# Seven block products for eight in four more places, and the last K tiles of a pair put last

## The chip, the cores and the metric

The kernel runs on one core of a Trainium2 chip. The metric is the device time of one execution in microseconds (us). The core has a matrix engine (TensorE, PE in the rows; its weight loads are PEld), a vector engine (VectorE, DVE), a scalar engine (ScalarE, ACT), a general engine (GpSimd, POOL) and a queue engine (SyncE, SP). Each works through its own queue in order; they wait for each other by semaphores. Weights and activations travel by DMA between device memory and the on-chip buffer, issued here from SP's and from POOL's queue.

## What is computed

Two blocks follow each other on x of 256 tokens x 2048 features, all in float32. The first block is two hybrid layers (banded attention, gated linear attention and attention to a memory). The change is in the second block, which in short is:

```python
h = rms_norm(x, norm_mix_pre)
proj = h @ w_in
a_q, a_f, a_i, a_g, b_q, b_k, b_v, b_f, g_a, g_b = jnp.split(proj, split_points, axis=-1)
y_a = hgrn2_mixer(a_q, a_f, a_i, a_g, lb, hgrn_norm_w) @ w_up_a
y_b = fox_mixer(b_q, b_k, b_v, b_f + b_fox_f) @ w_up_b
merged = sigmoid(g_a) * y_a + sigmoid(g_b) * y_b
x = x + rms_norm(merged @ w_o, norm_mix_post)
h = rms_norm(x, norm_ffn_pre)
gate, up = jnp.split(h @ w_ffn_in, 2, axis=-1)          # 2 x 5632 columns
x = x + rms_norm((silu(gate) * up) @ w_ffn_down, norm_ffn_post)
```

The HGRN2 mixer is a recurrence with a decay per feature, done in chunks of 64 tokens for 8 heads; the FoX mixer is a causal softmax attention with a forget gate, for 8 heads. g_a and g_b, the merge's gates, are 2048 columns each.

## The kernel before

**Products.** A float32 product is made of three matmuls on halves of less precision. Each operand x is split into a high part (a rounding copy) and a low part (x minus the high part), and `three` (L439) adds high·high, high·low and low·high into one accumulator (L441 to L443). For weights the high part is a cast on ACT (L356) and the low part a subtraction on DVE (L357); activations and other on-chip tiles are split the same way by `split_to` (L506, L507).

**Work units.** `Builder.run` (L249) goes through a list of jobs. A job is a group of up to 512 columns against all its K tiles of 128 rows, for the two token halves. It takes two K tiles at a time: one tile of weights (128 x 1024 floats, a "slot"), split into two slots, feeds 2 K tiles x 2 token halves x 3 = 12 matmuls of 128 x 512. Such a step is called a unit here. The accumulators of a job are a "main" tile of two banks, of which there are two; smaller products go to four single banks.

**Slots.** All tiles on chip of this size come from one pool of 41 slots. `ahead` (L370) loads raw weights on SP up to four ahead and splits up to six parts ahead of the unit that needs them, as long as enough slots are free. If they are not, `run` makes the split directly ahead of its unit, in the loop that begins with `while split <= i`. The order in which instructions are written down is the order of each engine's queue.

**Side work.** The heads of both mixers, the normalisations, the merging and the hidden activations are generators. `pump` (L229) advances up to two of them after each unit, by due times counted on a clock of matmul work. In the stretch of the merge's gates the HGRN heads (`hgrn_head`, L924) do, for each of two token halves of a head: the differences of the decays on POOL (`decay_levels`, L839: L846 to L856), two passes on ACT for the exponential (L857, L858), fourteen multiplications on POOL (L938, L939) and a reduction on DVE (L957), besides small products on PE. The FoX heads run in the same stretch, with their softmax on DVE and ACT (L786 to L791).

**Seven for eight.** `Shared` (L79) is a pair of two 512-column jobs a and b on the same activations. On one quad of K tiles (two K halves) the pair is a product of 2 x 2 blocks (token halves, K halves) with 2 x 2 blocks (K halves, the columns of a and of b): eight block products of 2 K tiles x 3 = 6 matmuls each. It is done with seven, by sums of blocks. The seven are called d, a, c, T1, T2, T4 and T3; the four T ones come after everything else of the pair. The sums of weight blocks are made by `sums` (L317) with four accumulating DMAs on POOL's queue (`add`, L303 and L304), each of which waits for the one before it: three (a += b, b += d, d += a) when a is split, and c += d when c is split. The raw tiles of the quad stay in their slots until the T products are split. The sums of activation blocks are made once per activation by `combos_of` (L616): four or five additions on POOL, one operation on DVE, and a split. The results leave the accumulators by copies on ACT (L462, L484, L491) and additions on DVE (L486 to L488, L493 to L497). Before, only the FFN's gate and up pairs do this, on K tiles 12 to 15.

**Order of the jobs.** gates gb0 to gb3 (each post, L1532, a tanh on ACT), the four jobs of w_up_b, gates ga0 to ga2, the last columns of w_in, ga3, w_up_a, then w_o (`residual_jobs`, L1614), then the FFN in three groups of 4, 4 and 3 pairs of 512 hidden columns, each followed by its part of w_ffn_down (four jobs; the last group's through `residual_jobs`).

Of the kernel before, what the change touches and what calls it, by code (L numbers as in the profile page):

```python
# [78 lines left out]
class Shared:  # L79
# [453 lines left out]
def network(ctx, tc, a):  # L533
# [82 lines left out]
    def combos_of(get2, quad):  # L616
# [13 lines left out]
        B.release([xi, ci])  # L630
        return ids

    def parted(ids):
# [893 lines left out]
    def post_gate(key, c):  # L1527
# [5 lines left out]
        return post  # L1533

    def post_upb(c):
        def post(ps):
# [29 lines left out]
    merging = {}  # L1566

    def merged(c):
# [4 lines left out]
        B.release([st[f"gb{c}"]])  # L1573

    def merged_get(kt):
# [7 lines left out]
    for g in range(2):  # L1583
# [29 lines left out]

    def residual_jobs(label, w_, post_row, resid, done, act_, order, k0=0, partial=None, pre1=None):  # L1614

# [31 lines left out]
        def finish(t):  # L1647
# [6 lines left out]
            done(q["r"], t)  # L1654

        n = len(order) // 2
        for c in range(4):
            jobs.append(Job("x", w_, 512 * c, 512, act_, post(c), order=order, k0=k0,
                            pre={0: begin, 1: pre1, 2: load_x}.get(c), apart=(label, n - 4 if c == 2 else 0, n) if c > 1 else None))

# [3 lines left out]
    def mix_done(ids, t):  # L1664
# [13 lines left out]
        else:  # L1678
            def done():
                B.release(ids + f["wi"])  # L1680
                f["make"] = make_fcombos()
                B.start(f["make"])
            start_late(fact, [f[0], f[1]], x1res, None, done, False)

    def pre_w2():
# [3 lines left out]
    residual_jobs("o", a["w_o_2"][0], a["norm_mix_post_2"][0], tokens(xres), mix_done, Act(merged_get), range(NKT),  # L1689
                  pre1=pre_w2)  # L1690

# [27 lines left out]

    QUADS = [(12, 13, 14, 15)]  # L1720

    def make_fcombos():
        for quad in QUADS:
            f.setdefault("combos", []).append(combos_of(lambda k: B.act[:, k:k + 2], quad))
            yield 3000

    def fcombos(q):
        if f["make"] in B.side:
            B.drain([f["make"]])
        return parted(f["combos"][q])  # L1730

    def post_both(c):

        def post(gi, ui):
# [3 lines left out]
            if f["units"] * 512 == D_FF:  # L1738
                B.release(sum(f["combos"], []))
        return post  # L1740

    def hidden(c, gi, ui=None):
# [15 lines left out]
        B.release([gi])  # L1758

    def hidden_get(kt):  # L1760
# [6 lines left out]

    def post_part(c, new):
        def post(ps):
            if c == 0 and new:  # L1770
                f["part"] = B.alloc(4)
            p = s(f["part"][c])
            if new:
                V.tensor_copy(p, flat(ps))
            else:
                V.tensor_tensor(p, p, flat(ps), ALU.add)
        return post

    def out_done(ids, t):
# [5 lines left out]
    for g, n in enumerate((4, 4, 3)):  # L1785
        for c in range(n):
            c0 = 512 * (at + c)
            head = (g, c) == (0, 0)
            if not head:
                std = range(16 - 4 * len(QUADS))  # L1790
                gate = Job("x", wf, c0, 512, fact, lambda ps: None, order=std, open=(1,))
                up = Job("x", wf, D_FF + c0, 512, fact, lambda ps: None, order=std)
                jobs.append(Shared(gate, up, QUADS, fact, fcombos, post_both(c)))
                continue
# [3 lines left out]
        if g < 2:  # L1798
            for c in range(4):
                jobs.append(Job("x", a["w_ffn_down_2"][0], 512 * c, 512, hact, post_part(c, g == 0), order=order, k0=k0))  # L1800
        else:
            residual_jobs("down", a["w_ffn_down_2"][0], a["norm_ffn_post_2"][0], tokens(x1res), out_done, hact, order, k0,
                          partial=lambda: f["part"])
        at += n
# [54 lines left out]
```

## Time and profile before

| | |
|---|---|
| median of 3 runs | 2400.83 us (2399.18 to 2401.85) |
| profiled execution | 2401.03 us |
| its span | 2399.3 us |
| PE busy | 2380.5 us, 99% of the span |
| DVE busy | 1566.2 us, 65% |
| ACT busy | 1160.0 us, 48% |
| POOL busy | 441.5 us, 18% |
| accumulating DMAs on POOL (L304) | 40, 512 KB each |

The span is the time from the first to the last record of the profile; the profiled execution's own time is 1.7 us longer. The busy time of PE counts matmuls whose ends are modelled and which overlap, so it is not a measure of how full the engine is; how far apart the starts of two matmuls are, tells more. The rows give start, duration, engine, line, operation, the tile written and the tiles read, and in square brackets the idle time of the engine ahead of the row and what ended it.

### The profile page before, as it was taken

To read this page: it belongs to the slowest core of one execution; us is meant where nothing else is said; L and a number is where in the kernel's file an instruction comes from. 1 tells how busy PE (TensorE), PEld (TensorE's weight loads), DVE (VectorE), ACT (ScalarE), POOL (GpSimd) and SP (SyncE) were. 2 spreads that over 40 slices of the span, in tenths; PEclk is the share of its full clock that TensorE was granted. 3 is DMA by queue.
4 is the path that set the end of the run, shared out by engine and by line. 5 is a ranking of instruction groups with operands and counts; after the bars stand their busy time and mean duration, and the time that the engine had idled before them with its cause. 6 is when DMAs were issued, how large, how long until landed. Compare 5 with 4: busy or idle time off the path is not lost. (4 is left out here: it accounts for less than half of the span.)

```text
span 2399.3 us, 31682 instructions
## 1 busy us (share of the span) xinstructions
PE 2380.5 (99%) x12045; PEld 2005.0 (84%) x12045; DVE 1566.2 (65%) x1783; ACT 1160.0 (48%) x1553; POOL 441.5 (18%) x646
## 2 busy tenths in 40 slices
PE   9999999999999999999999999999999999999998
PEld 7888888888888888888888888888888888888876
DVE  6587567566865667766775655657567557665675
ACT  5444455345454553655554434445555445544553
POOL 0330010004400110354754440001100000000000
PEclk9999999999999999999999999999999999999999
DMA  9545567674556574944654556675877578767773
GB/s 329 184 147 187 167 188 261 205 244 141 176 167 187 189 256 148 295 154 128 193 160 151 199 185 193 196 243 171 274 229 224 190 209 261 228 215 226 223 241 131
DMA packets 319672, 485.62 MB, mean 202 GB/s; under 512 B 22600, under 2 KB 162208, under 8 KB 319520
## 3 DMA queue, kind: packets, MB, share of 16 engines
q1 hardware_dynamic: 312528, 459.48, 58.8%
q0 software_dynamic: 6400, 23.07, 4.9%
q8 instruction: 94, 1.54, 0.3%
q10 hardware_dynamic: 592, 1.06, 0.1%
q14 instruction: 58, 0.48, 0.1%
HBM read 454.18 MB, written 8.40 MB: 193 GB/s over the span
## 5 line engine op out<-in xcount | busy, mean ns | idle before, releaser
L357 DVE TENSOR_TENSOR slot<-slot,slot 128x1024 fp32r<-128x1024 f32 x770 | 967.0, 1292 | 266.6 <-ACT slot L356 253.0
L356 ACT CAST slot<-slot 128x1024 fp32r<-128x1024 f32 x770 | 774.4, 1047 | 299.8 <-PE main L442 94.5
L428 PE MATMUL main<-act,slot 128*128 128x512 f32 x1824 | 651.2, 400 | 0.0
L441 PE MATMUL main<-slot,act 128*128 128x512 f32 x1488 | 589.5, 396 | 0.7 <-ACT slot L356 0.7
L442 PE MATMUL main<-slot,act 128*128 128x512 f32 x1488 | 580.0, 390 | 1.6 <-DVE slot L357 1.6
L443 PE MATMUL main<-slot,act 128*128 128x512 f32 x1488 | 580.3, 390 | 0.0
L429 PE MATMUL main<-act,slot 128*128 128x256 f32 x1824 | 510.0, 280 | 0.0
L428 PEld LDWEIGHTS main<-act,slot 128*128 128x128 f32 x1824 | 342.5, 188 | 80.3 <-issue 1.1
L429 PEld LDWEIGHTS main<-act,slot 128*128 128x128 f32 x1824 | 344.2, 189 | 0.8
L443 PEld LDWEIGHTS main<-slot,act 128*128 128x128 f32 x1488 | 279.3, 188 | 59.2
L442 PEld LDWEIGHTS main<-slot,act 128*128 128x128 f32 x1488 | 279.7, 188 | 58.3 <-DVE slot L357 2.8
L441 PEld LDWEIGHTS main<-slot,act 128*128 128x128 f32 x1488 | 279.6, 188 | 57.3 <-ACT slot L356 1.1
L441 PE MATMUL main<-slot,slot 128*128 128x512 f32 x620 | 244.2, 394 | 0.7 <-ACT slot L506 0.7
L443 PE MATMUL main<-slot,slot 128*128 128x512 f32 x620 | 242.6, 391 | 0.0
L442 PE MATMUL main<-slot,slot 128*128 128x512 f32 x620 | 242.1, 390 | 0.0
L304 POOL DMA_DIRECT2D slot<-slot x40 | 35.0, 874 | 563.4 <-DMA slot<-in_w_ffn_in_dram 196.8
L443 PEld LDWEIGHTS main<-slot,slot 128*128 128x128 f32 x620 | 116.8, 188 | 25.8 <-DVE slot L507 1.3
L441 PEld LDWEIGHTS main<-slot,slot 128*128 128x128 f32 x620 | 116.9, 188 | 25.3 <-ACT slot L506 1.4
L442 PEld LDWEIGHTS main<-slot,slot 128*128 128x128 f32 x620 | 116.8, 188 | 23.4
L507 DVE TENSOR_TENSOR slot<-slot,slot 128x1024 fp32r<-128x1024 f32 (+1 forms) x91 | 98.6, 1102 | 33.5 <-ACT slot L506 33.5
L846 POOL TENSOR_TENSOR slot<-slot 128x128 f32<-128x128 f32 x144 | 79.2, 581 | 192.3 <-PE main L428 93.2
L506 ACT CAST slot<-slot 128x1024 fp32r<-128x1024 f32 (+1 forms) x91 | 85.1, 956 | 47.0 <-DMA slot<-slot 16.5
(225 smaller groups left out, 1987.0 us busy)
## 6 DMA issues: line engine op xcount, KB each, us to landing
slot<-in_w_in_dram SPq DMA_DIRECT2D x384, 512.0 KB, 3.8
slot<-in_w_ffn_in_dram SPq DMA_DIRECT2D x176, 512.0 KB, 4.9
slot<-in_w_ffn_down_dram SPq DMA_DIRECT2D x88, 512.0 KB, 4.8
slot<-in_w_out_dram SPq DMA_DIRECT2D x64, 512.0 KB, 4.8
slot<-slot POOLq DMA_DIRECT2D x40, 512.0 KB, 7.2
slot<-in_w_o_dram SPq DMA_DIRECT2D x32, 512.0 KB, 4.7
slot<-in_w_mem_kv_dram SPq DMA_DIRECT2D x31, 512.0 KB, 6.4
slot<-in_w_up_b_dram SPq DMA_DIRECT2D x16, 512.0 KB, 4.6
```

The costliest lines, as they stand in the source:

```text
L304: nc.gpsimd.dma_start(self.s(out), self.s(x), accum_op=ALU.add)
L356: nc.scalar.copy(h, src)
L357: nc.vector.tensor_tensor(l, src, h.bitcast(F32), ALU.subtract)
L428: nc.tensor.matmul(job.ps[:, f, :], h[:, k, fs], xs, start=st, stop=False)
L429: nc.tensor.matmul(job.ps[:, f, :S], l[:, k, fs], xh, start=False, stop=en)
L441: nc.tensor.matmul(o, xh, h, start=start, stop=False)
L442: nc.tensor.matmul(o, xh, l, start=False, stop=False)
L443: nc.tensor.matmul(o, xl, h, start=False, stop=stop)
L506: nc.scalar.copy(h, src)
L507: nc.vector.tensor_tensor(l, src, h.bitcast(F32), ALU.subtract)
L846: G.tensor_tensor(view(E[:, l, :]), view(bt), ref, ALU.subtract)
```

## The change

- A pair's order (`Shared.sequence`): the last four K tiles of both jobs (two units each) are moved behind everything else but the T products. This holds for every pair, the FFN's too.
- `Combos` and `shared_pair` are new helpers: the sums of activation blocks as a generator, and a pair made of two jobs.
- Gates gb2 and gb3 become a pair, and ga0 and ga1, on K tiles 12 to 15, with sums of activation blocks that are made once when the second half of the FoX heads is started and kept until the second pair is done. Their tanh then works in place on the pair's results.
- w_o: columns 0 and 1 become a pair on K tiles 0 to 3.
- w_ffn_down: in the first and second group, columns 0 and 1 and columns 2 and 3 become pairs on the group's first four K tiles. In the third group columns 0 and 1 become a `Shared` without a quad: no product is left out, and only the order of the units differs.

```diff
@@ Shared.sequence
-        rest = slice(2, None)
-        seq = own(self.b, slice(0, 1)) + mine("d") + own(self.b, slice(1, 2)) + mine("a") + own(self.b, rest)
-        seq += own(self.a, slice(0, 1)) + mine("c") + own(self.a, slice(1, None))
+        seq = own(self.b, slice(0, 1)) + mine("d") + own(self.b, slice(1, 2)) + mine("a") + own(self.b, slice(2, -2))
+        seq += own(self.a, slice(0, 1)) + mine("c") + own(self.a, slice(1, -2))
+        seq += own(self.b, slice(-2, None)) + own(self.a, slice(-2, None))
...
+    def shared_pair(w_, cs, act_, order, combos, post, pres=(None, None), k0=0):
+
+        std = [k for k in order if k not in combos.quad]
+        ja, jb = (Job("x", w_, c, 512, act_, lambda ps: None, order=std, k0=k0, pre=pre, open=op)
+                  for c, pre, op in zip(cs, pres, ((1,), ())))
+        return Shared(ja, jb, [combos.quad], act_, combos, post)
...
     def start_f(g):
         B.drain([gens["bf"]])
+        if g == 1:
+            gcombos.start()
...
+    gcombos = Combos(lambda k: B.act[:, k:k + 2], (12, 13, 14, 15))
+
+    def post_gates(key, c, last):
+        def post(*ids):
+            for e, i in enumerate(ids):
+                st[f"{key}{c + e}"] = i
+                for t in range(2):
+                    A.activation(vt(i)[:, t, :], vt(i)[:, t, :], AF.Tanh, scale=rs2h[:, t:t + 1])
+            if last:
+                gcombos.release()
         return post
...
-    for c in range(4):
-        X(9224 + 512 * c, 512, act, post_gate("gb", c))
+    X(9224 + 512 * 0, 512, act, post_gate("gb", 0))
+    X(9224 + 512 * 1, 512, act, post_gate("gb", 1))
+    jobs.append(shared_pair(w, (9224 + 512 * 2, 9224 + 512 * 3), act, range(NKT), gcombos, post_gates("gb", 2, False)))
...
-    for c in range(3):
-        X(7176 + 512 * c, 512, act, post_gate("ga", c))
+    jobs.append(shared_pair(w, (7176 + 512 * 0, 7176 + 512 * 1), act, range(NKT), gcombos, post_gates("ga", 0, True)))
+    X(7176 + 512 * 2, 512, act, post_gate("ga", 2))
...
+        if combos:
+            jobs.append(shared_pair(w_, (0, 512), act_, order, combos, both, (pre1, begin), k0))
+        else:
+            one, two = (Job("x", w_, 512 * c, 512, act_, post(c), order=order, k0=k0, pre=pre)
+                        for c, pre in ((0, pre1), (1, begin)))
+            jobs.append(Shared(one, two, [], act_, None, None))
...
-            for c in range(4):
-                jobs.append(Job("x", a["w_ffn_down_2"][0], 512 * c, 512, hact, post_part(c, g == 0), order=order, k0=k0))
+            for c in (0, 2):
+                jobs.append(shared_pair(a["w_ffn_down_2"][0], (512 * c, 512 * c + 512), hact, order, Hidden(),
+                                        post_parts(c, g == 0), k0=k0))
```

The diff adds one line ahead of most of the code, so `decay_levels`' first line L846 is L875 after the change, L857 is L886, L304 is L305, and `three` is L442 to L444.

**The gates, POOL's queue.** slot_9910 holds a head's decays. Before, at the decay of a token half in gb2 (slot_11613), with the last multiplication of the half ahead of it:

```order
L944 TENSOR_TENSOR slot_11314<-slot_11314,slot_10191 128x128
L599 TENSOR_TENSOR rs_11608<-rs_11608,nhalf 128x1
L846 TENSOR_TENSOR slot_11613<-slot_9910 128x128 x6
L849 TENSOR_SCALAR slot_11613<-slot_9910 128x64
L850 COPY slot_11613<-slot_9910 128x64
L855 COPY slot_11613<-slot_9910 128x64
L856 TENSOR_SCALAR slot_11613<-slot_9910 128x64
L938 TENSOR_TENSOR slot_11613<-slot_11613,slot_9909 128x64
```

And now, where the same half is slot_11597, and slot_11403, 11379, 11330 and 11554 are the raw tiles a, b, d and c of the pair gb(2,3):

```order
L973 TENSOR_TENSOR slot_11311<-slot_11311,slot_10191 128x128
L305 DMA slot_11403<-slot_11379 128x1024
L305 DMA slot_11379<-slot_11330 128x1024
L305 DMA slot_11330<-slot_11403 128x1024
L875 TENSOR_TENSOR slot_11597<-slot_9910 128x128 x6
L878 TENSOR_SCALAR slot_11597<-slot_9910 128x64
L879 COPY slot_11597<-slot_9910 128x64
L884 COPY slot_11597<-slot_9910 128x64
L885 TENSOR_SCALAR slot_11597<-slot_9910 128x64
L600 TENSOR_TENSOR rs_11657<-rs_11657,nhalf 128x1
L305 DMA slot_11554<-slot_11330 128x1024
L967 TENSOR_TENSOR slot_11597<-slot_11597,slot_9909 128x64
```

Three accumulating DMAs now stand between the multiplications of one half and the decay of the next. In the second pair, ga(0,1), all four stand in a row ahead of the decay of slot_12429, and ACT's cast of slot_12442 (a unit of the pair's second accumulator, main_12510) behind that decay's exponentials.

**The gates, ACT's queue, at the same place.** Before (slot_11650 is a weight that PE uses four units later):

```order
L356 CAST slot_11586<-slot_11521 128x1024
L864 ACTIVATE sc_11511,ss_11607<-bank_11604 128x128
L857 ACTIVATE slot_11613<-slot_11613 128x1024
L858 ACTIVATE slot_11613<-slot_11613 128x1024
L796 COPY P_11402<-bank_11638 128x384
L356 CAST slot_11650<-slot_11527 128x1024
L356 CAST slot_11668<-slot_11546 128x1024
```

And now (slot_11610, 11662, 11681 and 11705 are weights of the pair's second accumulator, main_11635):

```order
L886 ACTIVATE slot_11597<-slot_11597 128x1024
L887 ACTIVATE slot_11597<-slot_11597 128x1024
L357 CAST slot_11610<-slot_11537 128x1024
L825 COPY P_11489<-bank_11648 128x384
L893 ACTIVATE sc_11545,ss_11656<-bank_11653 128x128
L507 CAST slot_11662<-slot_11554 128x1024
L507 CAST slot_11027<-bank_11675 128x256
L357 CAST slot_11681<-slot_11560 128x1024
L357 CAST slot_11705<-slot_11583 128x1024
```

PE's queue, now, at those weights; the units' other products are left out:

```order
L526 MATMUL bank_11629<-slot_11311 128x128 x4
L442 MATMUL main_11635<-slot_11610,act 128x512
...
L530 MATMUL bank_11648<-ident,P_11489 128x128 x3
L526 MATMUL bank_11653<-slot_8285,sc_11545 128x128
L526 MATMUL bank_11653<-slot_8285,cross_11547 128x128
L442 MATMUL main_11635<-slot_11662,act 128x512
...
L526 MATMUL bank_11675<-P_11428,slot_10537 128x128 x3
L442 MATMUL main_11635<-slot_11681,act 128x512
...
L526 MATMUL bank_11699<-slot_11311 128x128 x3
L526 MATMUL bank_11699<-slot_10191,slot_9909 128x128
L442 MATMUL main_11635<-slot_11705,act 128x512
```

Each of these weights is now cast after ACT or DVE has read a bank that PE fills directly ahead of the weight's unit. On DVE the subtractions of slot_11681 and slot_11705 stand behind such reads in the same way; that of slot_11786, five units on, stands behind a subtraction that reads a bank and behind the reduction of L986 (L957 before).

**The last group of down, PE's queue.** Before, column 0 is main_19495, and slot_19419 holds the last hidden columns, which are transposed here:

```order
L441 MATMUL main_19495<-slot_19453,slot_15408 128x512
...
L529 MATMUL bank_19576<-ident,slot_19419 128x128 x4
L529 MATMUL bank_19583<-ident,slot_19419 128x128 x4
L441 MATMUL main_19495<-slot_19467,slot_15752 128x512
```

And now, with column 0 in main_19821, column 1 in main_19748 and the last hidden columns in slot_19672:

```order
L442 MATMUL main_19748<-slot_19706,slot_15521 128x512
...
L442 MATMUL main_19821<-slot_19779,slot_15521 128x512
...
L530 MATMUL bank_19902<-ident,slot_19672 128x128 x4
L530 MATMUL bank_19909<-ident,slot_19672 128x128 x4
L442 MATMUL main_19748<-slot_19797,slot_15877 128x512
```

Four units of the second column now stand ahead of the transposes.

Counted over the whole program, PE has 42 matmuls fewer (11512 in place of 11554, as written down), DVE 81 more tensor-tensor operations, POOL 20 more, and POOL's queue 28 more DMAs.

## Rows read from the trace of the kernel before

**Rows 1.** The page: busy time and share of the span, for each engine

```profile
PE 2380.5 (99%) x12045; PEld 2005.0 (84%) x12045; DVE 1566.2 (65%) x1783; ACT 1160.0 (48%) x1553; POOL 441.5 (18%) x646
```

**Rows 2.** Waits of PE: what waited for what, total us, times, longest us

```profile
PE bank L529 <- DVE slot L1750: 2.5, 2, 1.4
PE bank L529 <- DVE sc L866: 1.7, 1, 1.7
```

**Rows 3.** PE's timeline in an FFN group's down, first and last of 46 products

```profile
1899.80 0.39 PE L441 MATMUL main<-slot,slot 128*128 128x512 f32 x1
...
1910.00 0.39 PE L441 MATMUL main<-slot,slot 128*128 128x512 f32 x1
```

**Rows 4.** PE's timeline in the last group, at the transposes

```profile
2329.04 0.39 PE L443 MATMUL main<-slot,slot 128*128 128x512 f32 x1
...
2332.27 0.99 PE L529 MATMUL bank<-ident,slot 128*128 128x128 f32 x7 [1.12 <-DVE slot L1750]
2333.49 0.50 PE L441 MATMUL main<-slot,slot 128*128 128x512 f32 x1 [0.24 <-ACT slot L506]
...
2337.35 0.40 PE L441 MATMUL main<-slot,slot 128*128 128x512 f32 x1
```

**Rows 5.** Stretches: length, busy PE, PEld, DVE, ACT, POOL, PEclk, DMA share, GB/s

```profile
2333.40:2337.40 4.00, 3.91 (x10) 2.82 (x11) 2.52 (x3) 1.47 (x3) 0.00 (x0) 0.57 0.54 203
...
1137.20:1141.00 3.80, 3.74 (x23) 3.23 (x23) 3.80 (x4) 2.85 (x4) 3.80 (x5) 1.00 0.86 259
```

**Rows 6.** The stretch of one FFN gate and up pair, columns as before

```profile
1796.70:1839.90 43.20, 43.20 (x196) 35.73 (x196) 31.32 (x34) 23.40 (x29) 3.52 (x4) 1.00 0.80 225
```

**Rows 7.** POOL's timeline over one FFN pair's accumulating DMAs

```profile
1972.93 0.87 POOL L304 DMA_DIRECT2D slot<-slot  x1 [32.15 <-DMA slot<-in_w_ffn_in_dram]
1978.75 0.87 POOL L304 DMA_DIRECT2D slot<-slot  x1 [4.95 <-PE main L442]
1988.57 0.87 POOL L304 DMA_DIRECT2D slot<-slot  x1 [8.96 <-DMA slot<-slot]
1996.98 0.87 POOL L304 DMA_DIRECT2D slot<-slot  x1 [7.54 <-issue]
```

**Rows 8.** POOL's timeline in gb2, at a decay

```profile
1304.59 0.55 POOL L599 TENSOR_TENSOR rs<-rs,nhalf 128x1 f32<-128x1 f32 x1 [9.82 <-DVE rs L598]
1305.10 2.21 POOL L846 TENSOR_TENSOR slot<-slot 128x128 f32<-128x128 f32 x6
```

**Rows 9.** ACT's timeline at the same place

```profile
1303.95 0.28 ACT L864 ACTIVATE sc<-bank 128x128 f32<-128x128 f32 x1 [3.61 <-PE bank L525]
...
1308.55 1.06 ACT L857 ACTIVATE slot<-slot 128x1024 f32<-128x1024 f32 x1 [4.23 <-POOL slot L856]
...
1310.97 1.05 ACT L356 CAST slot<-slot 128x1024 fp32r<-128x1024 f32 x1
```

**Rows 10.** DVE's timeline in gb2: a normalisation, a softmax's first row, the next

```profile
1287.95 0.29 DVE L866 TENSOR_TENSOR sc<-bank,rs 128x128 f32<-128x128 f32 x1 [0.69 <-POOL rs L599]
...
1289.88 0.29 DVE L786 CUSTOM_DVE_ANT_0 P<-bank,P 128x128 f32<-128x128 f32 x1
...
1292.65 1.23 DVE L357 TENSOR_TENSOR slot<-slot,slot 128x1024 fp32r<-128x1024 f32 x1
```

**Rows 11.** DMA issues: tiles, queue, count, KB each, median us to landing

```profile
slot<-in_w_in_dram SPq DMA_DIRECT2D x384, 512.0 KB, 3.8
...
slot<-slot POOLq DMA_DIRECT2D x40, 512.0 KB, 7.2
```

**Rows 12.** DVE by line, 1240 to 1470: count, busy us, mean ns, idle before

```profile
L357 DVE TENSOR_TENSOR slot<-slot,slot 128x1024 fp32r<-128x1024 f32 x76 | 93.4, 1251 | 31.6 <-ACT slot L356 31.2
L957 DVE TENSOR_REDUCE sc<-slot 128x128 f32<-128x1024 f32 x8 | 16.0, 2003 | 0.0
L954 DVE TENSOR_TENSOR slot<-bank,slot 128x512 f32<-128x512 f32 x16 | 11.0, 689 | 14.9 <-PE bank L525 14.9
```

**Rows 13.** ACT by line, the same stretch and columns

```profile
L506 ACT CAST slot<-bank 128x256 fp32r<-128x256 f32 x4 | 1.5, 371 | 7.0 <-PE bank L525 7.0
```

More of the change, by code (lines that the diff above doesn't have):

```diff
@@ L631, in combos_of, with __init__, start, gen @@
         return ids
+    class Combos:
+        def __init__(self, get2, quad):
+            self.get2, self.quad = get2, quad
+        def start(self):
+            def gen():
+                self.ids = combos_of(self.get2, self.quad)
+                yield
+            self.gen = gen()
+            B.start(self.gen)
+        def __call__(self, q):
+            if self.gen in B.side:
+                B.drain([self.gen])
+            return parted(self.ids)
+        def release(self):
+            B.release(self.ids)
+    def shared_pair(w_, cs, act_, order, combos, post, pres=(None, None), k0=0):
[3 more added lines that the diff above has]
+        return Shared(ja, jb, [combos.quad], act_, combos, post)
     def parted(ids):
@@ L1533, in post_gate @@
         return post
+    gcombos = Combos(lambda k: B.act[:, k:k + 2], (12, 13, 14, 15))
[7 more added lines that the diff above has]
+                gcombos.release()
+        return post
     def post_upb(c):
@@ L1566, in network @@
     merging = {}
+    FIRST = (0, 1, 2, 3)
+    ocombos = Combos(lambda k: B.act[:, k:k + 2], FIRST)
     def merged(c):
@@ L1573, in merged @@
         B.release([st[f"gb{c}"]])
+        if c == 1:
+            ocombos.start()
     def merged_get(kt):
@@ L1611, in network, with residual_jobs @@
                         pre=B.settle if c == 0 else None))
-    def residual_jobs(label, w_, post_row, resid, done, act_, order, k0=0, partial=None, pre1=None):
+    def residual_jobs(label, w_, post_row, resid, done, act_, order, combos, k0=0, partial=None, pre1=None):
         q = {}
@@ L1654, in finish, with both @@
             done(q["r"], t)
-        n = len(order) // 2
-        for c in range(4):
+        def both(i0, i1):
+            for c, i in enumerate((i0, i1)):
+                post(c)(vt(i))
+            B.release([i0, i1])
+            combos.release()
+        n = len(order) // 2
+        if combos:
[4 more added lines that the diff above has]
+            jobs.append(Shared(one, two, [], act_, None, None))
+        for c in (2, 3):
             jobs.append(Job("x", w_, 512 * c, 512, act_, post(c), order=order, k0=k0,
-                            pre={0: begin, 1: pre1, 2: load_x}.get(c), apart=(label, n - 4 if c == 2 else 0, n) if c > 1 else None))
+                            pre=load_x if c == 2 else None, apart=(label, n - 4 if c == 2 else 0, n)))
     fact = row_act(lambda: B.release(xsrc["ids"]))
@@ L1680, in done @@
                 B.release(ids + f["wi"])
-                f["make"] = make_fcombos()
-                B.start(f["make"])
+                fcombos.start()
             start_late(fact, [f[0], f[1]], x1res, None, done, False)
@@ L1689, in network @@
     residual_jobs("o", a["w_o_2"][0], a["norm_mix_post_2"][0], tokens(xres), mix_done, Act(merged_get), range(NKT),
-                  pre1=pre_w2)
+                  ocombos, pre1=pre_w2)
     wf = a["w_ffn_in_2"][0]
@@ L1718, in post_up2 @@
         return post
[L1720 to L1730, printed above, removed]
+    fcombos = Combos(lambda k: B.act[:, k:k + 2], (12, 13, 14, 15))
+    hcombos = []
     def post_both(c):
@@ L1738, in post @@
             if f["units"] * 512 == D_FF:
-                B.release(sum(f["combos"], []))
+                fcombos.release()
         return post
@@ L1758, in hidden @@
         B.release([gi])
+        if c == 1 and f.setdefault("groups", 0) < 2:
+            f["groups"] += 1
+            hcombos.append(Combos(lambda k: kx(f["h"][k // 2]), FIRST))
+            hcombos[-1].start()
     def hidden_get(kt):
@@ L1766, in network, with post_parts, post, __call__ @@
     hact = Act(hidden_get)
[L1768 to L1776, printed above, removed]
-        return post
+    def post_parts(c, new):
+        def post(*ids):
+            for e, i in enumerate(ids):
+                if new:
+                    f.setdefault("part", {})[c + e] = i
+                else:
+                    V.tensor_tensor(s(f["part"][c + e]), s(f["part"][c + e]), s(i), ALU.add)
+                    B.release([i])
+            if c == 2:
+                hcombos.pop().release()
+        return post
+    class Hidden:
+        quad = FIRST
+        def __call__(self, q):
+            return hcombos[-1](q)
     def out_done(ids, t):
@@ L1789, in network @@
             if not head:
[L1790 to L1793, printed above, removed]
+                jobs.append(shared_pair(wf, (c0, D_FF + c0), fact, range(NKT), fcombos, post_both(c)))
                 continue
@@ L1798, in network @@
         if g < 2:
-            for c in range(4):
-                jobs.append(Job("x", a["w_ffn_down_2"][0], 512 * c, 512, hact, post_part(c, g == 0), order=order, k0=k0))
-        else:
-            residual_jobs("down", a["w_ffn_down_2"][0], a["norm_ffn_post_2"][0], tokens(x1res), out_done, hact, order, k0,
-                          partial=lambda: f["part"])
+            for c in (0, 2):
+                jobs.append(shared_pair(a["w_ffn_down_2"][0], (512 * c, 512 * c + 512), hact, order, Hidden(),
+                                        post_parts(c, g == 0), k0=k0))
+        else:
+            residual_jobs("down", a["w_ffn_down_2"][0], a["norm_ffn_post_2"][0], tokens(x1res), out_done, hact, order, None, k0,
+                          partial=lambda: [f["part"][c] for c in range(4)])
         at += n
```

## The prediction

> **What bounds the kernel now.** I read the page's shares first, then who TensorE (PE) waits for, then PE's own timeline, and last what the queues beside it do in the merge's gates and in the FFN. PE is busy for 2380.5 of 2399.3 us [rows 1]; the longest waits in its list sum to a few us [rows 2]. So a product that is left out is worth its step, and a wait of PE its full length. A step of a 128x512 product is (1910.00 − 1899.80) / 45 = 0.227 us [rows 3].
>
> **What the change takes away.** Seven quads more go by seven block products for eight: two gate pairs, one output pair, four pairs of down. A block product is 2 K tiles × 3 = 6 matmuls, so 42 go: 42 × 0.227 = 9.5 us.
>
> The order of the last group's pair takes away a second thing. Before, PE stands ahead of the transposes of the hidden rows: from 2329.04 to 2333.49, 4.45 us, hold one product and eight transposes [rows 4]; a merged row in the same place gives 0.14 us for a transpose (0.99 for 7), so 4.45 − 0.23 − 1.1 = 3.1 us are waiting. Then nine products take 3.86 us (2333.49 to 2337.35) instead of 9 × 0.227 = 2.04, since the granted clock is 0.57 there [rows 4, 5]: 1.8 us. With the last four K tiles of both columns put last, four more units (48 products, 10.9 us) lie ahead of those transposes, over three times the wait. Gain 3.1 + 1.8 = 4.9 us; what is late next there is nothing that I find. Together **−14.4 us**.
>
> **What it adds without cost.** In o and down the pairs add the four accumulating transfers on GpSimd's (POOL's) queue, five POOL additions for the combinations, and DVE's additions. An FFN pair of before holds the same work: its 43.2 us have PE busy for all 43.2, with DVE at 31.3 and POOL at 3.5 [rows 6]. Nothing else waits on POOL's queue in o and down. I take 0; if DVE's 12 us of slack were gone, some us per pair.
>
> **What it adds in the gates: POOL's queue.** There a third party uses POOL: the HGRN heads' decays, which ACT turns into exponentials (L857, L858) before it goes on to the next weight cast in its queue. A sum of two tiles is a DMA on POOL, and each waits for the one before it: in an FFN chain the issues stand 5.8, 9.8 and 8.4 us apart, POOL doing nothing between them [rows 7]. In the gates of before POOL's decay takes 1305.10 to 1308.55 = 3.45 us, and ACT had waited 4.23 us for it [rows 8, 9]; this cost PE nothing, because the cast behind it (1310.97) made a weight that PE used four units later.
>
> In gb(2,3) the changed order puts three chained DMAs ahead of a decay, and right behind ACT's two exponentials the cast of slot_11610, which is the next accumulator's first weight. Counted from the score products of the head ahead (bank_11486):
> - DVE's softmax takes 1289.88 to 1292.65 = 2.8 and the subtraction behind it 1.2 [rows 10], then the first DMA may go: 4.0.
> - Two gaps. No row shows a chain in this stage. Such a DMA lands after 7.2 in the median; a weight load of this stage after 3.8 [rows 11]. Low end 3.8 + 0.87 for an issue = 4.7, high end 9.8 [rows 7]. I take 7.2, the row of the same kind of transfer: 14.4.
> - The third issue 0.87 [rows 7], the decay 3.45, two exponentials 2.1 (each 1.06), cast 1.05 [rows 8, 9], its low part 1.25 [rows 12], less one product, which needs only the high part: 8.5.
>
> Sum 26.9. PE's work until it needs the weight is 54 products (12.2) and nine small ones, at the transposes' 0.14, 13.5. **Wait 13.4** (8.4 to 18.6).
>
> In ga(0,1) four DMAs stand in a row ahead of a decay, and behind ACT's exponentials the cast of slot_12442. Counted from bank_12337: DVE's addition 0.69 and a subtraction 1.25 [rows 12], three gaps 21.6, then the same 8.5: 32.0; PE has 96 products and three small ones, 22.2. **Wait 9.8** (2.3 to 17.6).
>
> The Trainium skill's page "DMA: Bandwidth & Descriptors", section "Anatomy of one DMA — SWDGE (gpsimd) path", speaks against gaps this long: 2.0 us plus the bytes at 436 GB/s, an estimate of 3.2 us for 512 KB. The gaps of this trace [rows 7] are about two to three times that. By the page, with the issue added, the first wait would be 7.1 and the second 0.4.
>
> **What it adds in the gates: slots.** A pair parks its four raw tiles until the late products, holds a's split from early on, and takes four slots for results. The 41 slots then run out in gb(2,3): the order shows splits made directly ahead of their unit, behind operations that themselves wait for a PE product just ahead. Before, a split there lay about four units ahead. What PE then waits for, each from its last product ahead:
> - slot_11662: from 1303.95, where ACT starts on such a bank, to POOL's 1304.59 + 0.55, DVE's normalisation 0.29, subtraction 1.25, less 0.23: 2.5 [rows 8 to 10, 12].
> - slot_11681: ACT's 128x256 cast 0.37, cast 1.05, subtraction 1.25, less 0.23: 2.4 [rows 9, 12, 13].
> - slot_11705: DVE's addition 0.69, subtraction 1.25, less 0.23: 1.7 [rows 12].
> - slot_11786: ACT's cast 0.37, the subtraction of the same tile (taken as long), DVE's reduction 2.0, subtraction 1.25, less 0.4 for PE's work: 3.6 [rows 12, 13].
>
> Sum **10.2**. The low end leaves out what stands ahead of each split: four subtractions, less the product that needs only the high part, 4 × 1.02, and one cast, 5. I find none beyond these.
>
> **The clock.** After the scattered work at 2329 the next products ran 0.43 us apart, as at 1.2 instead of 2.4 GHz, 1.8 us lost [rows 4, 5]; after the 1.7 us wait at 1135 [rows 2] the clock stayed at 1.00 (3.74 busy of 3.80) [rows 5]. Both long waits are longer than the one at 2329: 2 × 1.8 = **3.6** (0 to 9, five such spells). The Trainium skill's page "TensorE: Matmul & The Clock Gate", section "HAM oscillation — how this bites in real kernels", has the engine throttle again after each wait in a loop; 2329 agrees, 1135 shows that a short one need not.
>
> **The sum.** Profiled time 2401.03 (span 2399.3 and 1.7 around it); −14.4 + 13.4 + 9.8 + 10.2 + 3.6 = +22.6 gives 2423.6. The median of the runs is 0.2 lower: **2423 us**. All low ends give 2401 − 14.4 + 8.4 + 2.3 + 5 = 2402, all high ones 2401 − 14.4 + 18.6 + 17.6 + 10.2 + 9 = 2442.
>
> **Rivals.**
> - *Faster: the weights arrive anyway.* In the FFN the same chains hold POOL's queue for over 20 us and PE waits for none of them [rows 6, 7]. If the gates behave so, only the gain is left: 2401.0 − 14.4 = 2386. Against it: the FFN has no decay in POOL's queue, so ACT never stands behind it. It decides at main_11635's first product: the chain would have to end 13 us sooner than by my sum.
> - *About the same: short gaps.* The gates have a gap near a weight load's (4.7): waits 8.4 and 2.3. With 5 for the slots and no clock lost, 2402; with 10.2, 2407 to 2408. For it: transfers in the FFN run beside DMA engines that are busy for 0.80 of the time [rows 6]. By the page on DMA (waits 7.1 and 0.4, slots 5 to 10): 2399 to 2404.
> - *Slower still: the clock.* If each of the six waits lowers the clock for a while, 6 × 1.8 = 10.8 instead of 3.6: 2431. For it the spell at 2333, against it 1135 [rows 5].
> - *Only part happens:* PE waits at POOL's queue but the splits are early enough: 2413.
>
> **How the numbers follow.** Forecast, both mechanisms (2409 to 2442, the rival of only one of them and that of the clock inside it): 0.66, of which 0.08 each for these two. Short gaps, 2396 to 2409: 0.14. Faster, 2384 to 2396: 0.18. Slower than 2442: 0.02. A range that should hold 8 in 10 takes the forecast, the short gaps and the upper edge of the gain: 2392 to 2442. A measurement of this kernel can tell some 0.2% from no change, 2396 to 2405.6. Faster 0.19; same 0.09 of the short gaps; slower 0.72.
>
> **What would show it.** Right: some 42 products fewer; no wait at the last group's transposes; PE idle for 8 to 18 us in gb(2,3) ahead of a unit whose cast follows L887 on ACT, POOL idle between three L305 rows ahead of a decay; a second such wait in ga(0,1); between them four waits of 2 to 4 us on subtractions at L358 or L508. Wrong: DMA issues in the gates under 5 us apart, or PE without a wait of over 3 us in the gates; or waits in the pairs of o and down, which I price at nothing.

## The result: 1.3% slower, and where the 31 us lie

The changed kernel takes 2431.93 us in the median of four runs (2431.42 to 2432.78), beside 2401.06 us before on the same chip (2399.18 to 2401.85). The ratio is 1.013, with a 95% interval of 1.0113 to 1.0148. The forecast was 2423 us, range 2392 to 2442, and slower with a chance of 0.72.

The page after: PE has the 42 records fewer that were expected (12045 to 12003 [rows 1]), and is busy about as long, while the span has grown from 2399.3 to 2430.0 us. So the time is in waits.

```profile
span 2430.0 us, 31846 instructions
...
PE 2379.3 (98%) x12003; PEld 2001.6 (82%) x12003; DVE 1633.2 (67%) x1864; ACT 1201.6 (49%) x1613; POOL 489.7 (20%) x694
```

Who PE waits for, after. The first two lines hold most of it. L530 is L529 of before: its line here holds the 1.7 us of [rows 2] and 12.4 us more, and the 2.5 us of [rows 2] ahead of the last group's transposes are gone.

```profile
PE main L442 <- ACT slot L357: 14.2, 4, 11.1
PE bank L530 <- DVE sc L895: 14.1, 2, 12.4
PE main L443 <- DVE slot L358: 6.5, 7, 1.8
```

The waits stand in two places. To size them I took, for every matmul of the trace, how far the start of the next one lies beyond the usual step of its shape, summed per 100 us. The stretch 1300 to 1400 has 30.5 us of that (1.2 before), 1400 to 1500 has 15.9 (1.4 before), and 2300 to 2400, where the last group lies, has 0.9 (5.3 before). The balance is 29.3 + 14.5 − 4.4 − 9.5 for the products = 29.9 of the 30.7 us by which the span grew. (The 9.5 us are those of the prediction, 42 steps; the others are read.)

**The first place, gb(2,3).** POOL's timeline, after: the three chained DMAs and the decay behind them (L875 is L846 of before). The gaps are 6.6 and 6.5 us, and POOL waits in them, as in the FFN [rows 7].

```profile
1296.81 0.95 POOL L305 DMA_DIRECT2D slot<-slot  x1 [5.79 <-DVE slot L508]
1303.40 0.86 POOL L305 DMA_DIRECT2D slot<-slot  x1 [5.64 <-DMA slot<-slot]
1309.92 0.85 POOL L305 DMA_DIRECT2D slot<-slot  x1 [5.66 <-DMA slot<-slot]
1310.50 2.49 POOL L875 TENSOR_TENSOR slot<-slot 128x128 f32<-128x128 f32 x6
```

ACT's timeline there. Its queue stands for 13.6 us on the decay, and the weight's cast comes right behind the two exponentials; before, the same wait was 4.23 us and nobody waited for it [rows 9].

```profile
1314.22 1.06 ACT L886 ACTIVATE slot<-slot 128x1024 f32<-128x1024 f32 x1 [13.60 <-POOL slot L885]
...
1316.27 1.03 ACT L357 CAST slot<-slot 128x1024 fp32r<-128x1024 f32 x1
```

PE's timeline from there on: the wait for that cast, and behind it the waits for the four splits that are made directly ahead of their units (slot_11662 at 1324.83 and 1326.19, slot_11681 at 1329.68 and 1331.19, slot_11705 at 1338.37, slot_11786 at 1348.82 and 1351.14; the first of a pair is the high part, the second the low part).

```profile
1317.35 0.80 PE L442 MATMUL main<-slot,act 128*128 128x512 f32 x1 [11.08 <-ACT slot L357]
1318.61 0.80 PE L443 MATMUL main<-slot,act 128*128 128x512 f32 x1 [0.46 <-DVE slot L358]
...
1324.83 0.50 PE L442 MATMUL main<-slot,act 128*128 128x512 f32 x1 [1.39 <-ACT slot L507]
1326.19 0.50 PE L443 MATMUL main<-slot,act 128*128 128x512 f32 x1 [0.86 <-DVE slot L508]
...
1329.68 0.51 PE L442 MATMUL main<-slot,act 128*128 128x512 f32 x1 [1.41 <-ACT slot L357]
1331.19 0.51 PE L443 MATMUL main<-slot,act 128*128 128x512 f32 x1 [1.00 <-DVE slot L358]
...
1338.37 0.50 PE L443 MATMUL main<-slot,act 128*128 128x512 f32 x1 [1.68 <-DVE slot L358]
...
1348.82 0.50 PE L442 MATMUL main<-slot,act 128*128 128x512 f32 x1 [1.35 <-ACT slot L357]
1351.14 0.51 PE L443 MATMUL main<-slot,act 128*128 128x512 f32 x1 [1.82 <-DVE slot L358]
```

**The second place, ga(0,1).** POOL's four DMAs, 6.5, 6.2 and 8.4 us apart. The first starts when a weight load (in_w_in_dram) has landed; the decay starts at 1439.83:

```profile
1418.09 0.94 POOL L305 DMA_DIRECT2D slot<-slot  x1 [3.73 <-DMA slot<-in_w_in_dram]
1424.62 0.86 POOL L305 DMA_DIRECT2D slot<-slot  x1 [5.59 <-DMA slot<-slot]
1430.84 0.86 POOL L305 DMA_DIRECT2D slot<-slot  x1 [5.36 <-DMA slot<-slot]
1439.27 0.86 POOL L305 DMA_DIRECT2D slot<-slot  x1 [7.57 <-issue]
```

ACT behind it, with the cast of slot_12442 and, behind the cast, the square sum (L893) of a head's output, which PE is about to transpose:

```profile
1443.56 1.06 ACT L886 ACTIVATE slot<-slot 128x1024 f32<-128x1024 f32 x1 [21.56 <-POOL slot L885]
...
1445.61 1.03 ACT L357 CAST slot<-slot 128x1024 fp32r<-128x1024 f32 x1
1446.54 0.27 ACT L893 ACTIVATE sc<-bank 128x128 f32<-128x128 f32 x1
```

PE's wait there ends with the normalisation (L895) of that output, not with the weight:

```profile
1449.09 0.45 PE L530 MATMUL bank<-ident,sc 128*128 128x128 f32 x1 [12.42 <-DVE sc L895]
```

**The clock.** Stretches after, columns as in [rows 5]: the two long waits (1306 and 1436), and PE right behind them at half the clock (0.52 and 0.50).

```profile
1306.00:1317.30 11.30, 0.27 (x3) 0.07 (x1) 0.00 (x0) 3.04 (x3) 4.26 (x11) 0.73 0.61 133
1317.30:1321.50 4.20, 3.69 (x8) 2.63 (x9) 1.83 (x2) 0.00 (x0) 0.00 (x0) 0.52 0.00 0
...
1436.20:1449.00 12.80, 0.47 (x3) 0.04 (x1) 1.64 (x4) 5.41 (x8) 5.21 (x14) 0.68 0.63 184
1449.00:1454.00 5.00, 4.91 (x12) 3.91 (x13) 5.00 (x5) 2.62 (x3) 5.00 (x4) 0.50 0.01 3
```

### The profile page after: what moved, and what is told of

The parts are those of the page before. It is cut to its first block, busy times and chain, and to the rows that moved or that the text cites. A ratio compares the mean times of both kernels' runs of the same rounds, so it can differ in the third digit from the quotient of the medians.

```text
span 2430.0 us, 31846 instructions
## 1 busy us (share of the span) xinstructions
PE 2379.3 (98%) x12003; PEld 2001.6 (82%) x12003; DVE 1633.2 (67%) x1864; ACT 1201.6 (49%) x1613; POOL 489.7 (20%) x694
## 5 line engine op out<-in xcount | busy, mean ns | idle before, releaser
L358 DVE TENSOR_TENSOR slot<-slot,slot 128x1024 fp32r<-128x1024 f32 x742 | 938.7, 1298 | 297.4 <-ACT slot L357 289.8
L357 ACT CAST slot<-slot 128x1024 fp32r<-128x1024 f32 x742 | 747.8, 1046 | 261.1 <-DVE slot L358 76.3
L442 PE MATMUL main<-slot,act 128*128 128x512 f32 x1452 | 578.2, 398 | 15.6 <-ACT slot L357 14.2
L443 PE MATMUL main<-slot,act 128*128 128x512 f32 x1452 | 569.1, 392 | 7.4 <-DVE slot L358 6.5
L444 PE MATMUL main<-slot,act 128*128 128x512 f32 x1452 | 568.8, 392 | 0.0
L442 PEld LDWEIGHTS main<-slot,act 128*128 128x128 f32 x1452 | 274.9, 189 | 72.2 <-ACT slot L357 15.2
L443 PEld LDWEIGHTS main<-slot,act 128*128 128x128 f32 x1452 | 274.7, 189 | 65.0 <-DVE slot L358 9.0
L444 PEld LDWEIGHTS main<-slot,act 128*128 128x128 f32 x1452 | 274.2, 189 | 58.1
L442 PE MATMUL main<-slot,slot 128*128 128x512 f32 x586 | 230.4, 393 | 0.7 <-ACT slot L507 0.7
L444 PE MATMUL main<-slot,slot 128*128 128x512 f32 x586 | 228.6, 390 | 0.0
L443 PE MATMUL main<-slot,slot 128*128 128x512 f32 x586 | 228.2, 389 | 0.0
L508 DVE TENSOR_TENSOR slot<-slot,slot 128x1024 fp32r<-128x1024 f32 (+1 forms) x144 | 166.3, 1170 | 79.6 <-ACT slot L507 79.0
L507 ACT CAST slot<-slot 128x1024 fp32r<-128x1024 f32 (+1 forms) x144 | 139.8, 989 | 113.2 <-DMA slot<-slot 67.3
L305 POOL DMA_DIRECT2D slot<-slot x68 | 59.6, 877 | 594.2 <-DMA slot<-slot 236.2
L444 PEld LDWEIGHTS main<-slot,slot 128*128 128x128 f32 x586 | 110.0, 188 | 24.3 <-DVE slot L508 1.3
L442 PEld LDWEIGHTS main<-slot,slot 128*128 128x128 f32 x586 | 110.0, 188 | 23.7 <-ACT slot L507 1.4
L443 PEld LDWEIGHTS main<-slot,slot 128*128 128x128 f32 x586 | 110.1, 188 | 22.2
L875 POOL TENSOR_TENSOR slot<-slot 128x128 f32<-128x128 f32 x144 | 79.4, 612 | 181.4 <-PE main L429 93.2
```

Source lines behind the costliest of these rows:

```text
L305: nc.gpsimd.dma_start(self.s(out), self.s(x), accum_op=ALU.add)
L357: nc.scalar.copy(h, src)
L358: nc.vector.tensor_tensor(l, src, h.bitcast(F32), ALU.subtract)
L442: nc.tensor.matmul(o, xh, h, start=start, stop=False)
L443: nc.tensor.matmul(o, xh, l, start=False, stop=False)
L444: nc.tensor.matmul(o, xl, h, start=False, stop=stop)
```

## The experiments

Each is built on the changed kernel, and each time is the median beside the kernel before on the same chip. Three theories stand against each other. *Queue and slots*, that of the prediction: POOL's queue, held by chained DMAs, delays decays, ACT's queue and the weights behind them, and the lack of slots makes splits late. *Transfers*: the 28 added DMAs crowd the others, in o and down too. *Bulk*: a pair brings more work beside its products than the gates can hide, whatever its order.

### All gates plain

The pairs gb(2,3) and ga(0,1) become plain jobs again; o, down and the orders stay.

```diff
-    jobs.append(shared_pair(w, (9224 + 512 * 2, 9224 + 512 * 3), act, range(NKT), gcombos, post_gates("gb", 2, False)))
+    for c in range(4):
+        X(9224 + 512 * c, 512, act, post_gate("gb", c))
...
-    jobs.append(shared_pair(w, (7176 + 512 * 0, 7176 + 512 * 1), act, range(NKT), gcombos, post_gates("ga", 0, True)))
+    for c in range(3):
+        X(7176 + 512 * c, 512, act, post_gate("ga", c))
```

> The changed kernel with the four gates of the two pairs as plain jobs again; o, down and the orders stay as changed. Queue and slots theory: all of the loss sits in the gates, so 30 products fewer (6.8 us) and the last group's wait and half clock gone (4.9) give 2401.1 - 11.7 = 2389; no wait of PE over 1 us between 1240 and 1480. Rival (the pairs of o and down pay too, by transfers on the same DMA engines): 2393 or more, with waits between 1650 and 2400.

Measured: 2388.86 us, before 2399.82, ratio 0.9954 (0.9939 to 0.9969). None of PE's waits lies in the gates; the longest in the list is the 1.7 us of [rows 2], ahead of them.

```profile
PE bank L530 <- DVE sc L895: 1.7, 1, 1.7
```

So the whole loss is in the two gate pairs, and the five other pairs with the new orders gain 11.0 us, where 11.7 were expected. The transfers theory falls for o and down: they keep 20 of the 28 added DMAs, and PE waits there for no more than before but for 0.2 us.

### One pair at a time

gb(2,3) alone (ga0 and ga1 plain), then ga(0,1) alone (gb2 and gb3 plain).

> The changed kernel with ga0 and ga1 as plain jobs again; the pair gb(2,3) stays. Queue and slots theory: the stretch 1300 to 1400 keeps its 29 us and the 14.5 us behind 1430 go, 36 products and 4.9 us are saved: 2401.1 - 8.2 - 4.9 + 29.3 = 2417. Rival (the second pair's wait is the first's passed on): both go on together, and the waits at the second pair's place would be seen in plain gates as well: 2425 or more.

Measured: 2418.34 us, ratio 1.0080 (1.0065 to 1.0095), as expected. The waits in gb(2,3) are those of the changed kernel, and the line of the normalisation falls back to the 1.7 us ahead of the gates:

```profile
PE main L442 <- ACT slot L357: 14.3, 4, 11.2
PE main L443 <- DVE slot L358: 7.7, 8, 1.8
...
PE bank L530 <- DVE sc L895: 1.7, 1, 1.7
```

> The changed kernel with gb2 and gb3 as plain jobs again; the pair ga(0,1) stays. Queue theory: one wait of some 12 us on POOL's queue with its half clock, none on splits: 2401.1 - 8.2 - 4.9 + 14.5 = 2402.5. Rival (the second wait needs the first pair's delay): 2388 to 2392.

Measured: 2397.03 us, ratio 0.9988 (0.9979 to 0.9997): slower than with all gates plain, by 8.2 us, where 13 were expected and the rival had 3 at most. The kind is the expected one, the size not. Here three DMAs, not four, stand ahead of the decay (L875); POOL's timeline shows them, and the line of PE's waits what they cost.

```profile
1386.49 0.96 POOL L305 DMA_DIRECT2D slot<-slot  x1 [9.11 <-DMA slot<-in_w_in_dram]
1392.15 0.86 POOL L305 DMA_DIRECT2D slot<-slot  x1 [4.70 <-DMA slot<-slot]
1400.29 0.86 POOL L305 DMA_DIRECT2D slot<-slot  x1 [7.28 <-issue]
1400.87 2.50 POOL L875 TENSOR_TENSOR slot<-slot 128x128 f32<-128x128 f32 x6
```

```profile
PE bank L530 <- DVE sc L895: 8.4, 2, 6.8
```

The wait at the transposes is 6.8 us with three DMAs and 12.4 with four, 5.6 us more for a chain that is 7.4 us longer from its first to its last issue (13.8 and 21.2). This is the nearest thing to a varied length of the chain that the runs hold, and it speaks for the chain. It is not a clean one, since the chain also starts at another point of PE's work. By the bulk theory the pair would have the same price in both kernels; it costs 8.2 us here and some 12 beside gb(2,3) (ratios 1.0130 and 1.0080).

### The sums on DVE

The four sums of weight tiles in the two gate pairs (`dve`) are additions on DVE; all other pairs keep the DMAs.

```diff
-            nc.gpsimd.dma_start(self.s(out), self.s(x), accum_op=ALU.add)
+            if dve:
+                nc.vector.tensor_tensor(self.s(out), self.s(out), self.s(x), ALU.add)
+            else:
+                nc.gpsimd.dma_start(self.s(out), self.s(x), accum_op=ALU.add)
```

> The changed kernel with the four sums of weight tiles in the two gate pairs done by additions on DVE (four of 128x1024 per pair) and not by DMAs on POOL's queue; FFN, o and down keep the DMAs. Queue theory: both waits on POOL's queue (11.3 and 12.6) and a half clock each (1.8) go, the waits on late splits (some 12 us, with their half clock) stay: 2431.9 - 27.5 = 2404. Rival (the slots alone, or DVE as the next bound): the place of the first wait keeps most of its 11 us, 2415 or more.

Measured: 2408.49 us, ratio 1.0035 (1.0023 to 1.0048), 23.4 us below the changed kernel by the medians. Both waits on POOL's queue are gone. Of the 4.5 us by which the expectation missed, most is a new wait: DVE's three additions stand ahead of a split whose unit PE reaches soon after (its first product starts at 1297.55). DVE's timeline: the additions (L307), a reduction, and the two subtractions behind them, the first of which PE waits 4.3 us for.

```profile
1295.17 3.86 DVE L307 TENSOR_TENSOR slot<-slot,slot 128x1024 f32<-128x1024 f32 x3
1298.95 1.88 DVE L992 TENSOR_REDUCE sc<-slot 128x128 f32<-128x1024 f32 x1
...
1301.02 2.38 DVE L362 TENSOR_TENSOR slot<-slot,slot 128x1024 fp32r<-128x1024 f32 x2
```

```profile
PE main L447 <- DVE slot L362: 9.9, 6, 4.3
```

The other waits are those on the four late splits, as they were: they do not hang on POOL's queue.

### The quad last

In the gate pairs (`self.dve`) the quad's products go last, so that its raw tiles are parked for a few units and not for the whole pair. Once with the sums on DVE, once with the DMAs.

```diff
+        if self.dve:
+            most, end = slice(0, -1), slice(-1, None)
+            seq = own(self.b, most) + own(self.a, most) + mine("d") + mine("a") + own(self.b, end) + mine("c") + own(self.a, end)
```

> The changed kernel with the gate pairs' sums on DVE and, in these two pairs, the quad's products put last (all units of both columns but one each first, then d, the two left units, c, a and the T products), so that raw tiles are parked shortly. Queue and slots theory: the waits on splits between 1310 and 1350 go, but for up to three at the end of gb(2,3), where the order still shows splits directly ahead of their unit (1 to 2 us each): 2388 to 2394. Rival (DVE's four additions per pair become the bound, or a pair costs more than it saves in the gates whatever its order): 2398 or more.

Measured: 2399.04 us, ratio 0.9998 (0.9989 to 1.0007). The waits that the run before had from 1302 on are gone, and waits at three units are left at the end of the pair (1326 to 1334, 0.8 to 2.1 us each), as expected; but a wait of 4.6 us came up among the late products, which the expectation did not have:

```profile
PE bank L449 <- ACT slot L492: 4.6, 1, 4.6
```

PE needs the bank that a copy on ACT (L492 here, L484 before) has yet to empty, and that copy stands in ACT's queue behind the exponentials of a decay. No DMA is in POOL's way here, yet the decay is late: by the profile POOL takes it up only when a product of PE is done, and its six differences (L884) take 7.82 us, where they took 2.21 in the gates of before [rows 8]. DVE makes four subtractions (L515) in the same time. Whether these slow POOL, no run tests.

```profile
1333.33 7.82 POOL L884 TENSOR_TENSOR slot<-slot 128x128 f32<-128x128 f32 x6 [15.21 <-PE main L451]
```

```profile
1334.09 5.45 DVE L515 TENSOR_TENSOR slot<-slot,slot 128x1024 fp32r<-128x1024 f32 x4
```

The number is the rival's: with both mechanisms of the prediction largely out of the way, the two pairs still cost 10 us against all gates plain (2388.86 on another chip). So the bulk theory has a part, which was not taken apart further.

> As the run with the quad last in the gate pairs, but with the sums by DMAs on POOL's queue. Slots theory: the waits on splits in the middle of gb(2,3) go here too. Queue theory: the chain of four DMAs, some 6.5 us apart, now begins only about 14 us ahead of the late products, so that PE waits for it there, 6 to 12 us in each pair, and for decays behind it: 2403 to 2415. Rival (the DMAs cost nothing once the splits come early): 2388 to 2394, as with the sums on DVE.

Measured: 2414.07 us, ratio 1.0061 (1.0046 to 1.0076). The same order with the DMAs costs 15 us more than with DVE. PE's two largest waits lie among the late products of gb(2,3), behind a split that ACT casts when the last DMA of the chain has landed (1346.09), and behind the decay in ga(0,1), for which ACT had stood 24.38 us:

```profile
PE bank L530 <- DVE slot L989: 8.7, 1, 8.7
PE main L446 <- ACT slot L361: 7.4, 2, 6.9
```

```profile
1346.09 1.99 ACT L511 CAST slot<-slot 128x1024 fp32r<-128x1024 f32 x2 [4.05 <-DMA slot<-slot]
...
1446.77 1.06 ACT L892 ACTIVATE slot<-slot 128x1024 f32<-128x1024 f32 x1 [24.38 <-POOL slot L891]
```

The bulk beside the products is the same in both kernels but for the place of the sums, so the 15 us are what the chain costs beyond the additions on DVE. That the DMAs cost nothing once splits come early is refuted.

### The last group's order undone

All gates plain, and columns 0 and 1 of the last group of down as plain jobs one after the other.

```diff
-            jobs.append(Shared(one, two, [], act_, None, None))
+            for c, pre in ((0, begin), (1, pre1)):
+                jobs.append(Job("x", w_, 512 * c, 512, act_, post(c), order=order, k0=k0, pre=pre))
```

> The kernel with all gates plain (2388.9) and, besides, the last group's columns 0 and 1 of down in the old order. Theory: the waits at the transposes (3.1) and the half clock behind them (1.8) come back: 2393.8. Rival (the half clock is paid elsewhere, or the wait has gone by other means): 2389 to 2391.

Measured: 2392.26 us, ratio 0.9968 (0.9957 to 0.9980): 3.4 us above the kernel with the new order (2388.86 on another chip, where the kernel before took 2399.82 beside 2399.93 here), where 4.9 were expected. The waits came back in full, the half clock did not:

```profile
PE bank L530 <- DVE slot L1797: 2.5, 2, 1.4
```

```profile
2325.90:2329.90 4.00, 3.95 (x16) 3.00 (x17) 2.51 (x3) 1.43 (x2) 0.00 (x0) 1.00 0.48 173
```

### A better version

ga(0,1) as a pair with its sums on DVE, gb2 and gb3 plain: there the slots suffice and POOL's queue is free.

> The changed kernel with gb2 and gb3 as plain jobs and the pair ga(0,1) with its sums on DVE. Theory: with slots to spare and POOL's queue free the pair gives what it saves, 6 products: 1.4 us below the kernel with all gates plain (2388.9), 2387.5. Rival (DVE's additions hold up a split, as the 4.5 us wait behind three of them in the run with both pairs): 2391 to 2393.

Measured: 2387.71 us, ratio 0.9949 (0.9933 to 0.9966), and none of PE's waits lies in the gates. To compare it with all gates plain on one chip, both were run again, with a third kernel in which ga2 and ga3 are a second such pair.

> The kernel with ga(0,1) alone as a pair on DVE, once more, beside the kernel with all gates plain on the same chip: theory, 1.4 us below that; rival, DVE's additions take it back: no difference.

> The kernel with all gates plain, once more, as the standard for the two kernels with ga pairs: 2388.9 if the chip is like the first one; theory, 1.4 and 2.7 us above those two, rival, within 0.5 us of them.

> gb0 to gb3 plain, ga(0,1) a pair with its sums on DVE, and ga2 and ga3, which lay apart, made a second such pair right behind it. Theory (a pair gives its six products where slots and queues leave it alone): 1.4 us below the kernel with one ga pair, 2386.3. Rival (the second pair meets the slots or the decays, as gb(2,3) did): 2388 or more, with a wait between 1430 and 1480.

Measured: one ga pair 2388.26 us, ratio 0.9950 (0.9938 to 0.9963); all gates plain 2389.15, 0.9953 (0.9941 to 0.9966); two ga pairs 2390.81, 0.9963 (0.9949 to 0.9976). The one pair was ahead of plain gates by 1.2 us the first time (on different chips) and 0.9 the second, but the intervals overlap, and 0.9 lies between theory and rival: it is likely, not shown, that it gives what its six products are worth. The second ga pair lost: its sums on DVE (L307) come in the middle of the first pair's results (L498), and ACT's tanh of the first pair waits 9.8 us for DVE, with the next weight casts behind it. PE's waits there sum to 3.2 us, the longest 1.1:

```profile
1441.51 3.74 DVE L307 TENSOR_TENSOR slot<-slot,slot 128x1024 f32<-128x1024 f32 x3
...
1447.44 0.68 DVE L498 TENSOR_TENSOR slot<-bank,slot 128x512 f32<-128x512 f32 x1
```

```profile
1449.48 2.56 ACT L1579 ACTIVATE slot<-slot,rs2h 128x512 f32<-128x512 f32 x4 [9.81 <-DVE slot L500]
1451.95 1.03 ACT L361 CAST slot<-slot 128x1024 fp32r<-128x1024 f32 x1
```

The version with one ga pair on DVE beats the kernel before by 0.5% and the changed one by 1.8%.

## Why the prediction was right, step by step

**The products.** 42 fewer, as counted. With the gates plain the gain came out 0.7 us below the sum of products and last group. In the run with the old last order, 30 products fewer and the new orders of the other pairs gave 7.7 us (2399.93 to 2392.26), where 30 steps are 6.8. The 12 of the gates were not priced apart from their waits.

**The wait on POOL's queue in gb(2,3): 13.4 expected, 11.5 measured (11.08 and 0.46).** The chain is the one of the prediction, link by link: from the softmax's first row to the first DMA 4.3 us (4.0), two gaps of 6.6 and 6.5 (7.2 each), from the third DMA to the end of the decay 4.3 (0.87 + 3.45), the exponentials and the cast as priced. The size that was off is mainly the gap, 1.3 of the 1.9 us. The whole kernel's median from issue to landing is now 6.3 us, not the 7.2 of [rows 11]:

```profile
slot<-slot POOLq DMA_DIRECT2D x68, 512.0 KB, 6.3
```

The Trainium skill's page "DMA: Bandwidth & Descriptors", in "Anatomy of one DMA — SWDGE (gpsimd) path", gives the prediction's estimate of 3.2 us for such a transfer. No accumulating DMA between tiles landed that fast here (4.5 us at the least, in the trace after), and the gaps of 4.8 to 8.4 us that the runs show in the gates are nearer to the trace of before.

**The wait in ga(0,1): 9.8 expected, 12.4 measured.** The weight's low part was ready 32 us after DVE took up its addition, as summed (1415.74 to 1447.90). That this part came out to 0.2 us owes something to luck: the first DMA waited for a weight load, which the sum did not have, and the gaps of 6.2 to 8.4 us only sum to about three times 7.2. And two things were wrong. PE was done at 1436.5, 1.4 us sooner than the sum had it (1415.74 + 22.2). And PE waited for something else: the transposes directly ahead of the weight's unit, whose input is normalised behind the same queue (square sum on ACT behind the cast, POOL's power behind the decay), 1.0 us later than the weight. I had followed the weight and not the small product ahead of it.

**The splits: 10.2 expected, 11.1 measured.** By unit, as the step of PE shows it beyond the usual: 2.7, 2.9, 1.9 and 3.6, beside 2.5, 2.4, 1.7 and 3.6. The run with the sums on DVE shows them apart from POOL's queue, and the run with plain gates shows them gone with the pair. That slots are what is short was read from the order; the quad put last parks tiles for less time and removes those of the middle, but as it changes the order too, slots alone were not isolated.

**The clock: 3.6 expected, 6.2 measured.** The trace after has 31 products of 128x512 more at a step of about 0.43 us than the kernel with plain gates, 0.2 us each. They lie in four spells: behind the two long waits, as expected, and behind two of the splits' waits. The Trainium skill's page "TensorE: Matmul & The Clock Gate", section "HAM oscillation — how this bites in real kernels", has the clock fall again after each wait in a loop. Four of the six places agree.

**The last group: 4.9 expected, 3.4 measured** by undoing it. The waits were right, the half clock behind them was not a fixed part of them.

**What I priced at nothing** in o and down was nothing: the plain-gates run has no wait there beyond those of before. The sum gave +22.6 for the profiled run, and the span grew by 30.7. Of the 8.1 between, the products and the last group are 0.5 (13.9 gained, not 14.4), the two long waits −1.9 and +2.6, the splits +0.9 and the clock +2.6, together 4.7. Of the remaining 3.4 us, 1.9 are three short waits that I had not listed (0.7 at 1298.9, 0.5 at 1368.4 and 0.6 at 1384.4); the rest is mostly in the first products behind the long waits, whose steps are long beyond the wait that is listed. Of the costs only the first long wait was put too high; the others were too low and the gain a little too high, so the sum is 8 us short of a time that the range held.

**The rivals.** *The weights arrive anyway* falls. That the FFN hides the same chain because no decay stands in POOL's queue there is the likely reason, and was not run. *Only part happens* falls too: both waits came. *The clock* had 2431 us, and 2431.9 were measured, but by chance: it had six spells of 1.8 us, and there were four of 6.2 us together, with the rest of the excess elsewhere. *Short gaps* was half a truth: gaps of 4.8 to 6 us were seen with the quad last, not in the changed kernel.

## What to carry to other kernels

Before adding work to a queue that is nearly idle, ask who else uses it and what is queued behind those users: POOL was busy for 18% of the time, and three chained DMAs there stopped ACT's queue and through it the weights. Where an engine is full, a saved product is worth its step only if each weight is ready some units ahead, so count what a new form parks on chip as well as what it saves. A sum that has a reader soon is cheaper on an engine with slack, even at 1.25 us each, than as a chain of transfers at 6.5 us; but such a burst has its own price for what is queued behind it.

## What the runs showed of the hardware

The two waits ahead of the last group's transposes, 2.5 us together, were of the same length before and in the run with the old order. In the one trace the products behind them ran at a granted clock of 0.57 [rows 5], in the other at 1.00. So waits of this size were followed by the lower clock in one trace and not in the other, and the 1.8 us that this cost in the one were no fixed price. Why the two differ was not followed. Behind each of the longest waits (4.3, 4.6 and 6.8 to 12.4 us in these runs) products followed at half the clock, 0.43 us apart.
